# A decoder step: the mask stored in reading order, the last layer's end by halves with filler products, late low parts on DVE alone

## The chip, the cores and the metric

The kernel runs on one core of a Trainium2 chip. The core has a matrix engine (TensorE, PE in the profile), three engines that work on 128 lanes (VectorE = DVE, ScalarE = ACT, GpSimd = POOL) and queues that move data between the chip's memory and SBUF. The engines run at the same time, each its own instructions in a fixed order; a semaphore holds an instruction until its inputs are there. The metric is the time of one execution on the device, in microseconds.

## The reference

Two groups of requests (512 prompt tokens, and 8 requests of 4 new tokens each, behind a cache of 2048) pass through two layers. Cut to what bears on this change:

```python
def trunk_layer(h, pe, pos, attn_fn, ...):
    z = h @ w_in
    a_u, a_v, q, k, v, qi, ki, wi = jnp.split(z, SPLIT_POINTS, axis=-1)
    ...
    b_out = attn_fn(q, k, v, qi, wi, ki)        # index scores, top-k keys, softmax
    mix = jnp.concatenate([a_out, b_out], axis=-1) @ w_o
    h = layer_norm(ALPHA * h + mix, ln1_g, ln1_b)
    ff = jnp.square(jax.nn.relu(h @ w_ff1)) @ w_ff2
    ple = jax.nn.sigmoid(h @ w_ple_gate) * (pe @ w_ple_proj)
    h = layer_norm(ALPHA * h + ff + ple, ln2_g, ln2_b)

def sample_sparse_attn(...):                    # for the 32 sample tokens
    I = indexer_scores(qi, wi, ki_all)          # against 2052 keys
    _, idx = lax.top_k(I, TOPK_SAMPLE)          # 256 of them
    return attend_selected(q, k_sel, v_sel, valid)
```

All is float32, the model width is 1024, the inner width of the MLP 4096.

## The kernel before

The 544 tokens lie as columns, in two halves of 272 (half 0 and half 1), features on the 128 partitions. Each float32 product is three products of rounded operands: a value is split into a high part `hi` (a cast, on ACT, L731) and a low part `lo` = value − `hi` (a subtraction, L735), and `mm3` issues hi·hi, lo·hi and hi·lo, 272 columns each. In the profile these carry the lines 828 to 833 (`mm`, `mm3`); here they are called bulk products. The first MLP matrix uses seven products for eight on 2 x 2 blocks; its operands (`Ah`, `Al`, `Bh`, `Bl`, `w` and `u` in the rows) are sums of the normalised columns that DVE, ACT and POOL make when a half's normalisation ends (L1929 and around).

Every weight comes as a chunk of 128 x 1024, by a DMA (`raw`); `splits` makes `hi` and `lo`. A chunk has a flag `g`, which the kernel before does not read: `Alt` at L734 lets the scheduler choose DVE (V) or POOL (G) for each low part.

The order of all instructions is not written out. Generators (`splits`, `backbone`, `s_attn_f`, ...) yield items: an instruction's engine and cost, an event, a buffer from a pool (`Al`), or alternatives. A list scheduler (`Sched`, L91) picks the item with the smallest start less a weight times the priority of its generator; the table `PR` holds these priorities, `WP` and `WO` the weights for PE and for the others, and `BIAS` and `GBIAS` what it adds to an alternative on DVE or POOL before it compares. What it picks is issued to its engine in that order, for good. So PE, like each engine, waits at the head of its row.

A layer goes: input projections and, among them, the index scores, the selection of the keys, softmax of the prompt blocks (`unit`, `head`) and of the sample tokens (`s_attn_f`); the output projection and first normalisation, half by half; the gate matrix `w_g`, in whose place PE works while the normalisation of the second half is made; then first and second MLP matrix in four steps (`STEPS`), and the second normalisation.

*The mask of the sample attention.* `s_scores` (L1358 to L1373) turns the selection into `maskb`, 128 x 513 bf16, 0 or a large negative number. `s_attn_f` lets PE add it to the scores: for four blocks `f`, four groups of four products with a stationary selector `sel` and 128 columns of `maskb`; the columns of one product lie 32 elements apart. A DVE instruction (L1826) takes each group from PSUM and reduces it.

*The end of a layer.* `F2` and `F2L` list outputs c and halves of the second MLP matrix; in the last of the four steps (q == 3) `F2L` gives outputs 0 to 4 in both halves in turn, then 5 to 7 in half 0, and 5 to 7 in half 1. `ln_apply` sums a half's columns with PE (products with `ones`), computes `mu`, `va`, `y` on DVE (tiny instructions, L861), spreads `mu` and `y` by products with `ident` over all partitions, and spawns `ln_col` for eight columns (L951, L953, L959), and in the last layer the stores.

Of the kernel before, what the change touches and what calls it, by code (L numbers as in the profile page):

```python
# [21 lines left out]
L = 2  # L22
# [29 lines left out]
F2L = F2[:7] + tuple(((c,), (h,)) for h in range(2) for c in (5, 6, 7))  # L52
STEPS = ((0, 5), (5, 9), (9, 13), (13, 16))
WARM = 9
GL = 1200.0
WP = 0.698
WO = 10.415
PR = {'q_sample': 10.5, 'free_raw': -0.5, 'gmix': 7.5, 'evac_c1': 11.5, 's_scores': 17.0, 's_block': 14.0, 'mix_b': 3.5, 'load_r': 8.5, 'kidx': 7.5, 's_attn': 3.0, 'evac_au': -2.5, 'head': 1.5, 's_kt': 6.0, 'loads': 3.0, 'evac_q': -4.0, 'sgu_load': 14.0, 's_relu': 1.5, 'mix_a': 14.5, 'setup1': 5.5, 's_attn_f': 12.5, 'gmlp': 4.5, 'unit': 0.0, 'load_pe': -1.5, 'evac_oa': 0.5, 'backbone': -6.5, 'evac_c0': -3.5, 'setup2': -1.5, 'splits': -2.5, 's_qk': 6.0, 'gnorm': 1.0, 'store': 7.0, 'setup': 6.0, 'wout22': 11.5, 'wadd': 12.0, 'mtee': 4.0, 'fin': 0.5, 'wsum': 7.0, 'wcopy': 0.5, 'evac_p': 10.0, 'ln1': 5.0, 'moving': -1.0, 'vload': 15.5, 'split_x': 12.0, 'evac_f2': -1.5, 'warm': 8.0, 'wsplit': 5.0, 'mv': 5.0, 'evac_o': 9.5, 'wout': 11.5, 'ln2': 10.5, 'evac_g': 6.0}
TBS = (3, 1, 2, 0)
BIAS = 65.107  # L60
GBIAS = 505.244
# [176 lines left out]
def cD(n, k=1):  # L238
    return ("V", (n / 0.96 + 70.0) * k, 1)
# [173 lines left out]
def build(tc, I, O, cols):  # L413
# [182 lines left out]
    for l in range(L):  # L596
# [9 lines left out]
        w["p"] = [chunk(I["w_p"][l, c], 1024, True) for c in range(2)]  # L606
# [95 lines left out]
    def splits():  # L702
        for c in splitq:
# [22 lines left out]
            for i, (a, b, le, re) in enumerate(c.parts):  # L726
# [7 lines left out]
                E = G if (yield Alt([cD(b - a)], [cG(b - a)])) else V  # L734
# [173 lines left out]

    def ln_apply(l, which, half, R, st, xi, dst):
# [5 lines left out]
        sq = st["q7", half]  # L915
        yield [("P", 640.0 * k)]
# [5 lines left out]
        S.free(sq)  # L922
        mu = sm(f"mu{half}", [128, 4])
# [327 lines left out]
    def s_scores(y):  # L1251
# [120 lines left out]
        yield [cW(513)]  # L1372
        V.tensor_scalar(y.maskb, rk[:, :513], -NEG, NEG, op0=ALU.mult, op1=ALU.add)  # L1373
# [440 lines left out]
    def s_attn_f(y, f, Pn, mx, nm, su, rs, vg, ob, fin):  # L1814
        for h2 in range(2):
            for qd in range(2):
                p = yield Al("at", [128, 512])
                yield [("P", 810.0)]
                mk = y.maskb[:, :512].rearrange("p (g h o t) -> p h t o g", h=2, o=8, t=2)
                for t4 in range(4):  # L1820
                    mm(p[:, t4 * 128:t4 * 128 + 128].rearrange("p (o g) -> p o g", o=8), sel[:, f, t4, :],
                       mk[:, h2, qd], True, True)
# [323 lines left out]
    def backbone():  # L2146
        for y in LY:
# [241 lines left out]
            if l + 1 < L:  # L2389
                S.spawn(kidx(LY[l + 1]), 1)  # L2390
# [54 lines left out]
```

## Time and profile before

| | |
|---|---|
| median of 3 runs | 1508.4 us (1508.12 to 1509.75) |
| the profiled execution's own time | 1493.62 us |
| its span, first to last instruction | 1491.9 us |
| mean granted TensorE clock | 0.983 |
| PE busy | 1438.7 us, 96% of the span |
| DVE busy | 1080.0 us, 72% |
| ACT busy | 808.5 us, 54% |
| POOL busy | 180.6 us, 12% |

The profile is of one execution, in microseconds from its first instruction. PE's share is high all the way; the two MLP stages (about 339 to 727 and 1078 to 1466) hold PE without a gap, and what PE idles lies in the attention stages, at the gate matrix, and at the end. In a timeline row, the number in brackets is how long the engine stood idle ahead of the instruction, and what released it; "x8" says that a row stands for eight instructions of one kind, with the time from the start of the first to the end of the last. Matmuls overlap, so what one costs is the distance from start to start.

### The profile page before, as it was taken

The page shows a single profiled execution, that of the slowest core. Times are in us where ns is not written, and L with a number is a line of the kernel's source. Part 1 is how long each engine was busy: PE and PEld are TensorE (multiplying, and loading weights), DVE is VectorE, ACT ScalarE, POOL GpSimd, SP SyncE. Part 2 cuts the span into 40 slices and gives each one's busy share as a digit, 9 for nine tenths or more (in the row PEclk, how much of TensorE's full clock was granted, in tenths as well). Part 3 has the DMA queues.
Part 4 walks back from the last instruction along what each step waited for, and adds up shares of the span by engine and source line. Part 5 has one row for each costly group of instructions (what it writes and reads, how often), then busy time and mean ns, then how long its engine had stood idle before and what let it go on. Part 6 is the DMA issues. An engine that isn't in the chain of part 4 may idle for free.

```text
span 1491.9 us, 31190 instructions
## 1 busy us (share of the span) xinstructions
PE 1438.7 (96%) x12262; PEld 1373.3 (92%) x12262; DVE 1080.0 (72%) x2807; ACT 808.5 (54%) x1893; POOL 180.6 (12%) x204
## 2 busy tenths in 40 slices
PE   9999999899999999999999998999899999999996
PEld 8798878899999999999987998779899999999996
DVE  5699976695955748566676999757869567484765
ACT  6678755473743616344466775754547345172543
POOL 2113511040000000000102044121400000000000
PEclk9999989999999999999999999999999999999998
DMA  7636424112231322313345354151122313222221
GB/s 239 216 100 221 131 100 175 41 43 86 99 128 57 128 72 85 127 58 117 113 129 181 102 198 144 71 187 34 68 72 100 128 58 114 84 101 100 72 71 61
DMA packets 55476, 164.48 MB, mean 110 GB/s; under 512 B 7648, under 2 KB 15008, under 8 KB 55328
## 3 DMA queue, kind: packets, MB, share of 16 engines
q1 hardware_dynamic: 44960, 124.73, 24.7%
q0 software_dynamic: 10368, 37.75, 7.5%
q8 instruction: 96, 1.57, 0.4%
q14 instruction: 52, 0.43, 0.1%
HBM read 156.09 MB, written 6.37 MB: 109 GB/s over the span
## 4 chain that ended last, share of the span: by engine, by line
PE 79%; DVE 11%; ACT 3%; DMA 3%; issue 2%; POOL 1%; POOLq 1%; SPq 0%; ACTq 0%; DVEq 0%
PE at L828 39%; PE mm L828 36%; DVE u L1235 2%; DVE m L1233 2%; PE at L1601 1%; PE at L1693 1%; DMA w<-in_cv,idxV 1%; POOLq L2427 1%; POOL lo L735 1%; DVE lo L735 1%; DMA raw<-in_w_au 1%; DVE t L953 1%; DVE t L951 1%; ACT hi L731 1%; DMA raw<-in_w_c 1%
## 5 line engine op out<-in xcount | busy, mean ns | idle before, releaser
L731 ACT CAST hi<-raw 128x1024 fp32r<-128x1024 f32 (+5 forms) x137 | 138.8, 1019 | 181.4 <-PE mm L828 93.4
L735 DVE TENSOR_TENSOR lo<-raw,hi 128x1024 fp32r<-128x1024 f32 (+5 forms) x131 | 155.6, 1189 | 30.2 <-ACT hi L731 29.6
L828 PE MATMUL mm<-Ah,hi 128*128 128x272 f32 x584 | 172.6, 296 | 0.9 <-DVE u L1899 0.4
L828 PE MATMUL mm<-Bh,hi 128*128 128x272 f32 x584 | 171.8, 294 | 1.5 <-DVE t L1014 1.3
L828 PE MATMUL mm<-Al,hi 128*128 128x272 f32 x584 | 169.4, 290 | 0.0
L828 PE MATMUL mm<-Bl,hi 128*128 128x272 f32 x584 | 168.9, 289 | 0.0
L828 PE MATMUL mm<-Ah,lo 128*128 128x272 f32 x584 | 168.8, 289 | 0.0
L828 PE MATMUL mm<-Bh,lo 128*128 128x272 f32 x584 | 168.6, 289 | 0.0
L828 PE MATMUL at<-w,hi 128*128 128x272 f32 x704 | 158.9, 289 | 0.0
L690 ACT CAST hi<-u 128x512 fp32r<-128x512 f32 x128 | 75.8, 619 | 97.0 <-PE mm L828 40.8
L828 PE MATMUL at<-w,lo 128*128 128x272 f32 x416 | 120.2, 289 | 0.0
L828 PEld LDWEIGHTS at<-w,hi 128*128 128x128 f32 x704 | 119.5, 188 | 0.0
L2073 DVE TENSOR_TENSOR u<-u,mm 128x272 f32<-128x272 f32 x96 | 41.9, 437 | 103.1 <-PE mm L828 102.9
L828 PEld LDWEIGHTS mm<-Bh,hi 128*128 128x128 f32 x584 | 110.7, 190 | 3.1 <-ACT wi L1145 1.7
L828 PEld LDWEIGHTS mm<-Ah,hi 128*128 128x128 f32 x584 | 110.7, 190 | 2.2 <-DVE u L1899 0.5
L690 ACT CAST hi<-raw 128x1024 fp32r<-128x1024 f32 x64 | 53.2, 831 | 109.2 <-PE at L828 35.4
L828 PEld LDWEIGHTS mm<-Ah,lo 128*128 128x128 f32 x584 | 110.8, 190 | 0.2
L828 PEld LDWEIGHTS mm<-Bh,lo 128*128 128x128 f32 x584 | 110.6, 189 | 0.1
L828 PEld LDWEIGHTS mm<-Al,hi 128*128 128x128 f32 x584 | 110.4, 189 | 0.0
L828 PEld LDWEIGHTS mm<-Bl,hi 128*128 128x128 f32 x584 | 110.2, 189 | 0.0
L828 PE MATMUL at<-Al,hi 128*128 128x272 f32 x376 | 108.8, 289 | 0.0
L828 PE MATMUL at<-Bl,hi 128*128 128x272 f32 x376 | 108.8, 289 | 0.0
(392 smaller groups left out, 4384.0 us busy)
## 6 DMA issues: line engine op xcount, KB each, us to landing
raw<-in_w_f SPq DMA_DIRECT2D x128, 512.0 KB, 3.3
raw<-in_w_q SPq DMA_DIRECT2D x16, 512.0 KB, 4.8
raw<-in_w_o SPq DMA_DIRECT2D x16, 512.0 KB, 3.4
raw<-in_w_g SPq DMA_DIRECT2D x16, 512.0 KB, 3.4
raw<-in_w_au SPq DMA_DIRECT2D x8, 512.0 KB, 3.4
raw<-in_w_av SPq DMA_DIRECT2D x8, 512.0 KB, 6.2
u<-in_x SPq DMA_DIRECT2D x8, 272.0 KB, 4.9
hD<-t SPq DMA_DIRECT2D x16, 136.0 KB, 4.2
```

Source lines behind the costliest of these rows:

```text
L690: A.copy(hi[:, :n], x)
L731: A.copy(c.hi[:, a:b], c.raw[:, a:b])
L735: E.tensor_tensor(c.lo[:, a:b], c.raw[:, a:b], c.hi[:, a:b].bitcast(F32), op=ALU.subtract)
L828: PE.matmul(out, l, r, start=start, stop=stop, skip_group_check=True)
L951: V.tensor_tensor(t[:, :n], r[:, a:b], pa[:, :n], op=ALU.subtract)
L953: V.tensor_tensor(t[:, :n], t[:, :n], pb[:, :n], op=ALU.mult)
L1233: V.max(m8, work[:, :N])
L1235: V.match_replace(work[:, :N], m8, work[:, :N], -3.3e38)
L1601: PE.transpose(p[:, c * 128:(c + 1) * 128], P[:, c * 128:(c + 1) * 128], ident)
L1693: PE.transpose(p[:, t, :], raw[:, (g * 4 + t) * 128:(g * 4 + t + 1) * 128], ident)
L2073: V.tensor_tensor(r[:, a:b], r[:, a:b], ps[:, :n], op=ALU.add)
L2427: with tile.TileContext(nc) as tc:
```

## The change

Five edits, two of which only reorder. (1) `PR`, `WP`, `WO` and `GBIAS` get other numbers, so the scheduler makes another order. (2) `maskb` is written in the order in which the products read it: two DVE instructions of 256 columns, read at a stride of 32 elements and written in a row, and one of a single column; the products then read 128 neighbouring columns. (3) In the last layer's last step, outputs 4 to 7 (not 5 to 7) go half by half (`F2E`). (4) `fill` issues products whose result nobody reads (`sel` by 512 columns of `maskb`): ten behind the last output of the last layer, and twelve when the sums of its last half are issued. (5) A low part may go to POOL only for chunks whose flag `g` is set; the flag goes from `w_p`, so DVE makes the low parts of `w_o`, `w_p`, `w_g`, and of the second MLP matrix.

```diff
+F2E = F2[:5] + tuple(((c,), (h,)) for h in range(2) for c in (4, 5, 6, 7))
-WP = 0.698
-WO = 10.415
-PR = {'q_sample': 10.5, 'free_raw': -0.5, ...
+WP = 0.928
+WO = 10.5
+PR = {'q_sample': 13.5, 'free_raw': 8.0, ...
-GBIAS = 505.244
+GBIAS = 422.464
-        w["p"] = [chunk(I["w_p"][l, c], 1024, True) for c in range(2)]
+        w["p"] = [chunk(I["w_p"][l, c], 1024) for c in range(2)]
...
-                E = G if (yield Alt([cD(b - a)], [cG(b - a)])) else V
+                E = G if c.g and (yield Alt([cD(b - a)], [cG(b - a)])) else V
+                if not c.g:
+                    yield [cD(b - a)]
...
+    def fill(pw, n, back):
+        for _ in range(n):
+            yield [("P", 215.0)]
+            mm(pw, sel[:, 0, 0, :], LY[0].maskb[:, :512], True, True)
+        if back is None:
+            S.free(pw)
+
     def ln_apply(l, which, half, R, st, xi, dst):
...
+        end = dst is not None and xi is None and half == 1
+        if end:
+            pw = yield Al("mm", [128, 512])
...
         S.free(sq)
+        if end:
+            S.spawn(fill(pw, 12, None), 0)
...
-        yield [cW(513)]
-        V.tensor_scalar(y.maskb, rk[:, :513], -NEG, NEG, op0=ALU.mult, op1=ALU.add)
+        src = rk[:, :512].rearrange("p (g h o t) -> p h t o g", h=2, o=8, t=2)
+        dst = y.maskb[:, :512].rearrange("p (h t o g) -> p h t o g", h=2, o=8, t=2)
+        for h in range(2):
+            yield [cX(256)]
+            V.tensor_scalar(dst[:, h], src[:, h], -NEG, NEG, op0=ALU.mult, op1=ALU.add)
+        yield [("V", 70.0, 1)]
+        V.tensor_scalar(y.maskb[:, 512:513], rk[:, 512:513], -NEG, NEG, op0=ALU.mult, op1=ALU.add)
...
-                mk = y.maskb[:, :512].rearrange("p (g h o t) -> p h t o g", h=2, o=8, t=2)
                 for t4 in range(4):
-                    mm(p[:, t4 * 128:t4 * 128 + 128].rearrange("p (o g) -> p o g", o=8), sel[:, f, t4, :],
-                       mk[:, h2, qd], True, True)
+                    mm(p[:, t4 * 128:t4 * 128 + 128], sel[:, f, t4, :],
+                       y.maskb[:, (2 * h2 + qd) * 128:(2 * h2 + qd + 1) * 128], True, True)
...
-                for cs, hs in F2L if q == 3 else F2:
+                for cs, hs in F2 if q < 3 else F2E if l == L - 1 else F2L:
...
             if l + 1 < L:
                 S.spawn(kidx(LY[l + 1]), 1)
+            else:
+                pw = yield Al("mm", [128, 512])
+                yield from fill(pw, 10, None)
```

The changed file is longer, so its lines have higher numbers: L735 is L738 there, L861 L864, L951 L966, L1601 L1621, L1929 L1948, L2087 L2106.

*POOL at the gate matrix of layer 0.* POOL's order before (`lo688` and `lo753` are low parts of chunks of `w_g`, `Bl` operands of the first MLP matrix):

```order
L1929 TENSOR_TENSOR u657_4084<-u390_2547,w656_4083 128x272
L1929 TENSOR_TENSOR u657_4084<-u391_2550,w656_4083 128x272
L735 TENSOR_TENSOR lo688_4241<-raw592_3693,hi686_4233 128x1024
L1929 TENSOR_TENSOR u658_4085<-u395_2582,w656_4083 128x272
L1929 TENSOR_TENSOR Bl655_4082<-u390_2547,Bh654_4081 128x272
L1929 TENSOR_TENSOR Bl655_4082<-u391_2550,Bh654_4081 128x272
L1929 TENSOR_TENSOR Bl655_4082<-u392_2559,Bh654_4081 128x272
L735 TENSOR_TENSOR lo753_4645<-raw676_4199,hi736_4514 128x1024
```

and now:

```order
L1948 TENSOR_TENSOR u657_4086<-u370_2427,w656_4085 128x272
L1948 TENSOR_TENSOR u657_4086<-u371_2429,w656_4085 128x272
L1948 TENSOR_TENSOR u658_4087<-u374_2444,w656_4085 128x272
L1948 TENSOR_TENSOR u658_4087<-u378_2460,w656_4085 128x272
L1948 TENSOR_TENSOR Bl655_4084<-u370_2427,Bh653_4082 128x272
L1948 TENSOR_TENSOR Bl655_4084<-u371_2429,Bh653_4082 128x272
L1948 TENSOR_TENSOR Bl655_4084<-u374_2444,Bh653_4082 128x272
L909 TENSOR_TENSOR u1350_8859<-u1350_8859,t1399_9347 128x272
```

Both low parts are gone from POOL; it does one more subtraction of operands.

*DVE at the same place.* Before, from the third low part of `w_g` to the normalisation of half 0 (`y0`: its inverse deviation; L951: the normalisation itself):

```order
L735 TENSOR_TENSOR lo711_4419<-raw603_3771,hi700_4338 128x1024
L2087 TENSOR_SCALAR u712_4428<-mm713_4429 128x272
L861 SCALAR_TENSOR_TENSOR tmp0_4325<-tmp0_4325 92x3
L861 SCALAR_TENSOR_TENSOR y0_4324<-tmp0_4325,y0_4324 92x3
L861 TENSOR_TENSOR tmp0_4325<-y0_4324 92x3
L861 TENSOR_TENSOR tmp0_4325<-tmp0_4325,va0_4323 92x3
L861 SCALAR_TENSOR_TENSOR y0_4324<-tmp0_4325,y0_4324 92x3
L2087 TENSOR_SCALAR u717_4450<-mm718_4451 128x272
L735 TENSOR_TENSOR lo719_4454<-raw667_4153,hi715_4437 128x1024
L951 TENSOR_TENSOR t726_4487<-u390_2547,at721_4471 128x272
```

and now, up to the same place:

```order
L864 SCALAR_TENSOR_TENSOR tmp0_4327<-tmp0_4327,va0_4325 92x3
L864 SCALAR_TENSOR_TENSOR tmp0_4327<-tmp0_4327 92x3
L738 TENSOR_TENSOR lo720_4461<-raw667_4155,hi716_4440 128x1024
L2106 TENSOR_SCALAR u721_4471<-mm722_4472 128x272
L864 SCALAR_TENSOR_TENSOR y0_4326<-tmp0_4327,y0_4326 92x3
L864 TENSOR_TENSOR tmp0_4327<-y0_4326 92x3
L864 TENSOR_TENSOR tmp0_4327<-tmp0_4327,va0_4325 92x3
L864 SCALAR_TENSOR_TENSOR y0_4326<-tmp0_4327,y0_4326 92x3
L738 TENSOR_TENSOR lo732_4508<-raw676_4201,hi726_4494 128x1024
L966 TENSOR_TENSOR t735_4521<-u370_2427,at733_4510 128x272
```

Four low parts, `lo688`, `lo711`, `lo720` and `lo732` (before: two, `lo711` and `lo719`), now stand on DVE ahead of the normalisation; three of them stand between `mu0` and the last step of `y0`, where one stood. On PE the broadcast of `mu0` and `y0` moves from row 1802 of its order to row 1820, and so does that of layer 1, from 6908 to 6926; the product that reads the last low part (`lo753`, now `lo732`) stays at row 1961.

*PE at the mask of layer 0.* Before, two mask groups (of four, of which the last and the first product are shown) and the transposes between them:

```order
L828 LDWEIGHTS sel_111
L828 MATMUL at479_3027<-maskb_137,sel_111 128x128
L1435 MATMUL at477_3019<-identR_106,u357_2318 128x128 x4
L828 LDWEIGHTS sel_111
L828 MATMUL at480_3034<-maskb_137,sel_111 128x128
```

and now:

```order
L831 MATMUL at475_3046<-maskb_137,sel_111 128x128
L1621 MATMUL at478_3063<-ident_101,u461_2932 128x128 x2
L1455 MATMUL at477_3050<-identR_106,u409_2650 128x128 x4
L831 MATMUL at476_3048<-u450_2914,u3_127 64x128
L831 MATMUL at476_3048<-u452_2916,u3_127 64x128
L831 MATMUL at479_3065<-u451_2915,u3_127 64x128
L831 MATMUL at479_3065<-u453_2917,u3_127 64x128
L831 LDWEIGHTS sel_111
L831 MATMUL at480_3071<-maskb_137,sel_111 128x128
```

816 bulk products of the layer stand ahead of the first mask product of 128 columns, and 774 before. Between it and the transposes of the sample tokens' softmax stood 27 before, and none stands now, nor between these and the products with the values. In layer 1 some 70 bulk products that stood ahead of the mask stand in and behind it now.

*PE at the end.* Before, the last of the sums of half 1 and the broadcasts:

```order
L828 MATMUL at2814_18719<-ones_99,u2132_13757 92x1
L828 MATMUL at2814_18719<-ones_99,u2759_18137 92x1
L828 MATMUL at2814_18719<-ones_99,t2813_18713 92x1
L828 MATMUL at2815_18744<-ident_101,mu1_4108 128x92 x3
L828 MATMUL at2816_18745<-ident_101,y1_4110 128x92 x3
```

and now, the last fillers ahead of the broadcasts and one behind them:

```order
L831 MATMUL mm2816_18729<-maskb_137,sel_111 128x512
L831 LDWEIGHTS sel_111
L831 MATMUL mm2813_18720<-maskb_137,sel_111 128x512
L831 MATMUL at2817_18768<-ident_101,mu1_4110 128x92 x3
L831 MATMUL at2818_18769<-ident_101,y1_4112 128x92 x3
L831 LDWEIGHTS sel_111
L831 MATMUL mm2813_18720<-maskb_137,sel_111 128x512
```

Of the 22 fillers, seven stand between the last bulk product and the sums, 13 between the sums and the broadcasts, and two behind.

## Rows read from the trace of the kernel before

**Rows 1.** Part 1 of the page: each engine's busy time, share and instructions.

```profile
PE 1438.7 (96%) x12262; PEld 1373.3 (92%) x12262; DVE 1080.0 (72%) x2807; ACT 808.5 (54%) x1893; POOL 180.6 (12%) x204
```

**Rows 2.** What PE waited for: in all us, times, longest us.

```profile
PE mm L828 <- POOL lo L735: 10.8, 2, 5.4
PE at L1601 <- DVE u L1597: 7.0, 6, 3.3
PE at L828 <- DVE maskb L1373: 1.6, 1, 1.6
```

**Rows 3.** Timeline of POOL in layer 0: start us, us, engine, line, out<-in.

```profile
301.66 2.37 POOL L735 TENSOR_TENSOR lo<-raw,hi 128x1024 fp32r<-128x1024 f32 x1
324.34 14.46 POOL L735 TENSOR_TENSOR lo<-raw,hi 128x1024 fp32r<-128x1024 f32 x1 [5.32 <-ACT hi L731]
```

**Rows 4.** Timeline of PE in layer 0; in brackets the idle time and its releaser.

```profile
338.85 0.60 PE L828 MATMUL mm<-w,lo 128*128 128x272 f32 x1 [5.39 <-POOL lo L735]
```

**Rows 5.** Windows of layers 0 and 1: us, busy us by engine, granted clock, DMA.

```profile
324.00:334.00 10.00, 9.46 (x76) 9.24 (x74) 10.00 (x30) 4.80 (x14) 9.66 (x1) 1.00 0.00 0
339.00:343.00 4.00, 4.00 (x22) 4.00 (x23) 0.00 (x0) 0.00 (x0) 0.00 (x0) 0.65 0.71 261
1077.45:1083.45 6.00, 6.00 (x30) 6.00 (x31) 0.08 (x1) 0.51 (x2) 0.00 (x0) 0.58 0.52 179
```

**Rows 6.** Timeline of DVE in the gate stage of layer 0.

```profile
305.51 0.14 DVE L861 TENSOR_SCALAR mu<-at 92x3 f32<-92x3 f32 x1
309.38 1.22 DVE L735 TENSOR_TENSOR lo<-raw,hi 128x1024 fp32r<-128x1024 f32 x1
311.63 0.16 DVE L861 SCALAR_TENSOR_TENSOR y<-tmp,y 92x3 f32<-92x3 f32 x1
```

**Rows 7.** Timeline of PE in the same stage: half 0's broadcast of the mean.

```profile
312.25 0.80 PE L828 MATMUL at<-ident,mu 92*128 92x92 f32 x6
```

**Rows 8.** Timeline of PE, mask products (layer 1) and transposes (layer 0), with their successors.

```profile
209.03 0.79 PE L1435 MATMUL at<-identR,u 128*128 128x128 f32 x8
209.66 0.36 PE L828 MATMUL mm<-Ah,hi 128*128 128x272 f32 x1
956.29 1.90 PE L828 MATMUL at<-maskb,sel 128*128 128x128 bf16 x8
958.02 0.61 PE L1601 MATMUL at<-ident,u 128*128 128x128 f32 x4
```

**Rows 9.** Window of layer 0's mask products.

```profile
198.00:210.00 12.00, 12.00 (x68) 9.62 (x67) 8.95 (x29) 6.07 (x13) 0.00 (x0) 0.57 0.00 1
```

**Rows 10.** Timeline of DVE ahead of the mask, layers 0 and 1.

```profile
191.59 2.32 DVE L1367 SCALAR_TENSOR_TENSOR u<-u,rem,t 128x513 f32<-128x513 f32 x1
194.67 0.43 DVE L1373 TENSOR_SCALAR maskb<-u 128x513 bf16<-128x513 f32 x1
930.12 0.75 DVE L1367 SCALAR_TENSOR_TENSOR u<-u,rem,t 128x513 f32<-128x513 f32 x1
```

**Rows 11.** Timeline of PE at the end: sums and broadcasts of both halves.

```profile
1463.90 0.57 PE L828 MATMUL at<-ones,u 128*92 128x1 f32 x6
1465.64 0.30 PE L828 MATMUL at<-ones,t 128*92 128x1 f32 x2
1468.89 0.80 PE L828 MATMUL at<-ident,mu 92*128 92x92 f32 x6
1476.49 0.94 PE L828 MATMUL at<-ones,u 128*92 128x1 f32 x6 [1.59 <-DVE u L904]
1479.44 1.59 PE L828 MATMUL at<-ident,mu 92*128 92x92 f32 x6 [0.25 <-DVE mu L861]
1481.37 1.59 PE L828 MATMUL at<-ident,y 92*128 92x92 f32 x6 [0.34 <-DVE y L861]
```

**Rows 12.** Timeline of PE, products of 512 columns and one, layer 1.

```profile
927.07 0.38 PE L828 MATMUL at<-t,gall 128*128 128x512 f16 x2
927.31 0.38 PE L828 MATMUL at<-t,gneg 128*128 128x512 f16 x2
```

More of the change, by code (lines that the diff above doesn't have):

```diff
@@ L55 @@
 GL = 1200.0
-WP = 0.698
-WO = 10.415
-PR = {'q_sample': 10.5, 'free_raw': -0.5, 'gmix': 7.5, 'evac_c1': 11.5, 's_scores': 17.0, 's_block': 14.0, 'mix_b': 3.5, 'load_r': 8.5, 'kidx': 7.5, 's_attn': 3.0, 'evac_au': -2.5, 'head': 1.5, 's_kt': 6.0, 'loads': 3.0, 'evac_q': -4.0, 'sgu_load': 14.0, 's_relu': 1.5, 'mix_a': 14.5, 'setup1': 5.5, 's_attn_f': 12.5, 'gmlp': 4.5, 'unit': 0.0, 'load_pe': -1.5, 'evac_oa': 0.5, 'backbone': -6.5, 'evac_c0': -3.5, 'setup2': -1.5, 'splits': -2.5, 's_qk': 6.0, 'gnorm': 1.0, 'store': 7.0, 'setup': 6.0, 'wout22': 11.5, 'wadd': 12.0, 'mtee': 4.0, 'fin': 0.5, 'wsum': 7.0, 'wcopy': 0.5, 'evac_p': 10.0, 'ln1': 5.0, 'moving': -1.0, 'vload': 15.5, 'split_x': 12.0, 'evac_f2': -1.5, 'warm': 8.0, 'wsplit': 5.0, 'mv': 5.0, 'evac_o': 9.5, 'wout': 11.5, 'ln2': 10.5, 'evac_g': 6.0}
+WP = 0.928
+WO = 10.5
+PR = {'q_sample': 13.5, 'free_raw': 8.0, 'gmix': 7.5, 'evac_c1': 14.0, 's_scores': 17.0, 's_block': 17.5, 'mix_b': 4.5, 'load_r': 6.5, 'kidx': 7.5, 's_attn': 5.0, 'evac_au': -2.5, 'head': 1.5, 's_kt': 6.0, 'loads': 7.5, 'evac_q': -4.0, 'sgu_load': 13.5, 's_relu': 1.0, 'mix_a': 14.5, 'setup1': 8.5, 's_attn_f': 10.5, 'gmlp': 4.5, 'unit': 9.0, 'load_pe': 13.0, 'evac_oa': -0.5, 'backbone': -5.5, 'evac_c0': -3.5, 'setup2': -2.0, 'splits': -2.5, 's_qk': 3.5, 'gnorm': 3.0, 'store': 3.0, 'setup': 13.0, 'wout22': 11.5, 'wadd': 12.0, 'mtee': 4.0, 'fin': 0.5, 'wsum': 7.0, 'wcopy': 0.5, 'evac_p': 10.0, 'ln1': 2.0, 'moving': 11.5, 'vload': 2.5, 'split_x': -1.0, 'evac_f2': 0.0, 'warm': 7.5, 'wsplit': 6.0, 'mv': 5.0, 'evac_o': 9.5, 'wout': 11.5, 'ln2': 10.5, 'evac_g': 0.0}
 TBS = (3, 1, 2, 0)
 BIAS = 65.107
-GBIAS = 505.244
+GBIAS = 422.464
 DMARGIN = 1200.0
@@ L1817, in s_attn_f @@
                 p = yield Al("at", [128, 512])
-                yield [("P", 810.0)]
-                mk = y.maskb[:, :512].rearrange("p (g h o t) -> p h t o g", h=2, o=8, t=2)
+                yield [("P", 300.0)]
                 for t4 in range(4):
-                    mm(p[:, t4 * 128:t4 * 128 + 128].rearrange("p (o g) -> p o g", o=8), sel[:, f, t4, :],
-                       mk[:, h2, qd], True, True)
+                    mm(p[:, t4 * 128:t4 * 128 + 128], sel[:, f, t4, :],
+                       y.maskb[:, (2 * h2 + qd) * 128:(2 * h2 + qd + 1) * 128], True, True)
                 sv = y.S[:, f, h2, qd * 4:qd * 4 + 4].rearrange("p a b c -> p (a b c)")
```

## Prediction

> **What bounds the kernel now.** I first read the busy shares and then what TensorE (PE) waits for, since PE is busy 1438.7 us of the span of 1491.9 us [rows 1]. The reader is to see there that only 53 us of the span are PE's to win back, and that anything else must make PE's own products shorter. The list of PE's waits shows one big entry: two waits of 5.4 us each, for a low part (`lo`) that POOL makes at L735; the others are for DVE and far smaller [rows 2].
>
> The timeline of POOL shows what this low part is. The same instruction, 128 rows by 1024 columns, takes 2.37 us at 301.66 and 14.46 us at 324.34 [rows 3]. While it runs in its long form, DVE is busy 10.00 us of 10 [rows 5], with subtractions and sums that read two operands from SBUF. PE stands in its fixed order before the product that reads this low part and starts again at 338.85 [rows 4]. The windows behind it show a second price: the granted clock, 1.00 while PE streamed, is 0.65 in the mean over the 4 us after the first stall, and 0.58 over the 6 us after the second, in layer 1 [rows 5]; a mean between the levels of 1.2 and 2.4 GHz.
>
> The other places that the change touches: the mask products, eight of which take 958.02 − 956.29 = 1.73 us, 0.216 us each, where eight transposes of as many columns take 209.66 − 209.03 = 0.63 us, 0.079 each [rows 8]; and the end, where PE waits for DVE three times and runs its broadcasts at 1.59 us where the half before took 0.80 [rows 11].
>
> **Low parts on DVE only.** Removed: both stalls, 2 × 5.39 = 10.8 us [rows 2, 4], and the slow clock behind them, 4 × (1 − 0.65) = 1.4 us and 6 × (1 − 0.58) = 2.5 us [rows 5]. Together −14.7. Added: in each layer DVE makes two more low parts, at 1.22 us each [rows 6], and they stand, with two more evacuations of a product, between `mu0` and the last step of `y0`. For an evacuation I estimate 0.35 us, by 272 of the 1024 columns of a low part. That chain took 311.63 − 305.51 = 6.1 us before [rows 6]. Now it gets 2.4 + 0.7, less one subtraction (0.35) that moves out: 2.7 to 2.8 us longer, so `y0` ends near 314.5. The first broadcast of `mu0` and `y0` started at 312.25 [rows 7], and the new order puts 18 products ahead of it, at 0.13 us each (76 in 10 us, [rows 5]) 2.3 us. It then comes to 314.6, and its second half, which is what needs `y0`, some 0.6 us later. So the longer chain is just covered: I take a wait of 0.5 us in each layer. If the cover is gone altogether, the 2.7 us stand bare in both layers, +5.4. Term: −14.7 + 1.0 = **−13.7**, with ends −9.3 and −14.7. What is late next is DVE: `lo732` now stands ahead of the normalisation of half 0, and what this half feeds begins 2.3 us later; but PE reads `lo732` only at its row 1961, as it did `lo753`, 141 rows behind the broadcast, about 19 us.
>
> By the Trainium skill ("SBUF — State Buffer", Who interferes with whom) DVE and GpSimd share one pair of ports as an exclusive lock, and a DVE instruction with two SBUF inputs keeps a GpSimd instruction that reads SBUF out altogether. The 14.46 against 2.37 us agrees. By that rule the four POOL subtractions (L1948) that stay in the stage would now meet the four low parts on DVE, and each could be kept out for one of them, 1.22 us.
>
> **The mask in reading order.** 64 of the 80 mask products read 128 columns a long way apart. Read in a row they should cost what the transposes do, which are fp32r and not bf16, but the nearest rows: 64 × (0.216 − 0.079) = 8.8 us if PE sets the pace and has the full clock. PE does set it in layer 0: it is busy 12.00 us of 12 from 198 to 210, at a mean granted clock of 0.57 [rows 9]. But DVE, which takes each group of four with a reduction, is busy 8.95 of these 12 us [rows 9]: it allows 3.0 us in layer 0 at most, while its work stays in the stretch. In layer 1 products of the projections stand between, and 32 × 0.137 = 4.4 can nearly all be had; I take 3.5. Term: **−6.5**; the ends are 0 (DVE sets the pace everywhere) and −11 (8.8, and 2 us of clock).
>
> The write of the mask becomes two instructions of 256 columns and one of one column in place of one of 513 at 0.43 us [rows 10]. From that row, and 0.16 for the smallest DVE instructions (the last of `y0`, [rows 6]), 0.43 + 0.16 + 0.16 makes +0.3 a layer on a chain for which PE already waited 1.6 us once [rows 2]. In that chain stood also the one instruction of 2.32 us whose twin in layer 1 took 0.75 [rows 10]; a POOL low part ran beside it, and this goes, −1.6 in layer 0. In layer 1 the order now puts some 70 bulk products less between the selection and the mask: I give back 0.5 there. Term **−0.6**, from −1.6 to +3.
>
> The skill's page "SBUF — State Buffer" (SBUF "cachelines", under Door 1: The DMA port swizzle) says that accesses that leave a 16-byte line each pay. DVE now reads the mask at a stride of 32 fp32 values, as PE did before. By the rule DVE would pay there what PE saves: at PE's own ratio of 0.216 to 0.079 the write grows from 0.43 to 1.2 us. The trace before has no such DVE read, so it can only be bounded; the upper end of +3 covers two of them with both waits.
>
> **The last layer's end.** The last product ends at 1476.49 − 1.59 = 1474.90; the sums start 1.59 later, the broadcast of `mu` at 1479.44 takes 1.59, that of `y` starts at 1481.37 and takes 1.59, so it ends at +8.06 [rows 11]. The clock falls in between. The nearest row for a filler is a pair of 512 columns and one: 927.31 − 927.07 = 0.24 [rows 12], so 0.215 for 512. Seven stand before the sums: 1.5 us, as long as the wait they fill. The sums take 2.0, as they did for the half before, from 1463.90 to 1465.94 (for this half 2.95, at a falling clock) [rows 11], to +3.5. Then 13 more stand ahead of the broadcast, since PE keeps its order: 2.8 us, to +6.35, when `mu` and `y` are there already (from the end of the sums to the broadcast of `y` DVE took 1.9 us, so `y` is there by +5.5). With two broadcasts of 0.80, as for the half before [rows 11], the end is at +7.95. Term **−0.1**: the fillers hold the broadcast up by as much as the clock gives back. The far end: the clock falls all the same, 13 × 0.43 + 2 × 1.59, +4. The half-by-half order of four outputs moves no product off PE; it only lets half 0's normalisation end 3 us earlier.
>
> **The new order.** Nothing of PE's amount of work changes except 22 fillers. In layer 0, 42 bulk products stand ahead of the mask that stood in or behind it: 5 us of cover that the softmax chains between mask and outputs no longer have, but one of the waits of those chains (7.0 us in six waits [rows 2]) lies at the very end, and units that start earlier shorten it. I take 0, ±5.
>
> Sum: −13.7 − 6.5 − 0.6 − 0.1 = −20.9. The profiled execution's own time is 1493.62 us (1491.9 and 1.7 around it), so 1472.7 for such an execution. It is 14.8 us under the median of the runs shown, and I carry that distance on: 1508.4 − 20.9 = 1487.5, **1488**.
>
> **Rivals.**
> A, DVE becomes the bound at the gate. `y0` misses its broadcast by 2.7 us in both layers, or the POOL subtractions are kept out for as long: for it, DVE is full from 324 to 334; against it, the 18 products. −9.3 for the term, 1492.
> B, the mask products were not PE's pace: the reductions on DVE (busy 75% there [rows 9]) take their place, and the term is near 0: −14.4, 1494.
> C, the attention loses its cover. In layer 0 no bulk product stands between the first mask product and the value products; PE, in order, waits at the transposes of a softmax that DVE has not scaled. That is the wait of 3.3 us that stands once now [rows 2]; it decides when it comes some six times more in the two layers, 21 us, which eats all: 1508 to 1514. For it, DVE's chains are long and 42 and some 70 products left; against it, the same products are still done somewhere, and cover waits that exist.
> D, the low part on POOL was only the last of several late things, and PE meets another 3 us later: each stall keeps 2 to 3 us of its 5.4, and the clock falls all the same: 1498.
>
> **How the numbers follow.** The forecast within ±4: 0.45. A 0.15, B 0.15, D 0.10, C 0.07, and 0.08 for more than the forecast (clock and order both give). The range 1475 to 1501 leaves out C and the ends of the others, some 0.15 to 0.2. A difference under 0.2%, 3 us, is about what a measurement of this kernel cannot tell from none. Faster by more: all but C and a mixture of D with lost cover, 0.87. Within 0.2%: 0.06. Slower: 0.07.
>
> **What the changed profile would show.** Right: no PE wait on POOL at L738, the granted clock 1.00 from 333 to 345; PE's wait for `y` in the broadcast under 1 us; mask products at 0.08 us; a broadcast of `mu` at 0.8 us near the end, starting right behind a filler. Wrong: a wait of PE on DVE `y` or `Bl` of 2 us and more in the gate stage (A), mask groups that follow each other at DVE's 0.7 us (B), new waits at L1621 of 3 us (C), broadcasts at 1.59 us again in the end.

## The result: 1471.8 us, below the range

The changed kernel takes 1471.76 us in the median (1470.9 to 1472.45, four runs) against 1508.88 (1508.12 to 1509.75) for the kernel before: a ratio of 0.9758, with a 95% interval of 0.9742 to 0.9774. The forecast was 1488 with a range of 1475 to 1501: the direction was right, the gain of 37 us is 1.8 times the 20.9 forecast. The profiled executions tell another story: 1493.62 before and 1471.24 after, 22.4 us apart, 1.5 us from the sum. The changed kernel's profiled execution stands at its median; that of the kernel before stood 15 us below its own. So the sum as a whole held for the execution from which it was read, and what went wrong is how it was carried to the median. Most of what follows is about these 15 us.

First the page of the changed kernel, its line of busy times and that of the chain that ended last (before, DVE had 11% of that chain and POOL 1%):

```profile
PE 1427.5 (97%) x12284; PEld 1363.9 (93%) x12284; DVE 1083.2 (74%) x2812; ACT 805.4 (55%) x1895; POOL 143.8 (10%) x201
PE 79%; DVE 15%; ACT 3%; issue 1%; DMA 1%; another core or an unknown queue 0%; SPq 0%; DVEq 0%; ACTq 0%
```

and two of PE's waits (us in all, times, longest), the largest and the only one on a low part:

```profile
PE at L1621 <- DVE u L1617: 4.6, 3, 3.3
PE mm L831 <- DVE lo L738: 0.9, 2, 0.5
```

No wait on POOL is left. At the two gate matrices, where [rows 2] had 10.8 us, PE does not wait for a low part at all; the 0.9 us are two waits in the input projections, at 123.4 and 850.0 us, and come with the new order (b_tables, below, has them too). PE is busy 11 us less than in [rows 1].

The gate stage of layer 0, PE's broadcast first, then the last step of `y0` and the last low part on DVE:

```profile
312.24 0.80 PE L831 MATMUL at<-ident,mu 92*128 92x92 f32 x6
312.87 0.83 PE L831 MATMUL at<-ident,y 92*128 92x92 f32 x6
312.12 0.16 DVE L864 SCALAR_TENSOR_TENSOR y<-tmp,y 92x3 f32<-92x3 f32 x1
313.03 1.23 DVE L738 TENSOR_TENSOR lo<-raw,hi 128x1024 fp32r<-128x1024 f32 x1 [0.75 <-ACT hi L732]
```

They answer to [rows 6, 7]. `y0` ends at 312.28, and the broadcast that needs it starts at 312.87: the longer chain is covered by the 18 products, with 0.6 us to spare. The broadcast stands at the same instant as before with 18 products more ahead of it, so PE came to this stage 2.3 us earlier. `mu0` came as much earlier (303.24, before 305.51), and the chain from it to the end of `y0` takes 9.0 us where it took 6.3: the 2.7 to 2.8 us more of the forecast. The windows behind answer to [rows 5]:

```profile
326.00:333.00 7.00, 7.00 (x57) 6.84 (x56) 7.00 (x21) 3.83 (x10) 0.00 (x0) 1.00 0.00 0
333.00:345.00 12.00, 12.00 (x97) 11.95 (x96) 10.83 (x21) 5.35 (x8) 0.00 (x0) 1.00 0.48 146
1063.00:1080.00 17.00, 17.00 (x137) 17.00 (x137) 12.09 (x22) 4.98 (x11) 0.00 (x0) 1.00 0.45 149
```

The granted clock stays at 1.00 through both gate stages, though DVE is as full ahead of layer 0's as before (7.00 us of 7).

The mask of layer 0, answering to [rows 8, 10]: eight mask products and what follows on PE, then on DVE the instruction that took 2.32 us and the new write of the mask, and the wait that PE has some microseconds later:

```profile
203.83 0.62 PE L831 MATMUL at<-maskb,sel 128*128 128x128 bf16 x8
204.28 0.39 PE L1621 MATMUL at<-ident,u 128*128 128x128 f32 x2
186.49 0.76 DVE L1382 SCALAR_TENSOR_TENSOR u<-u,rem,t 128x513 f32<-128x513 f32 x1
188.49 0.75 DVE L1391 TENSOR_SCALAR maskb<-u 128x256 bf16<-128x256 f32 x2
189.16 0.14 DVE L1393 TENSOR_SCALAR maskb<-u 128x1 bf16<-128x1 f32 x1
212.90 1.85 PE L1621 MATMUL at<-ident,u 128*128 128x128 f32 x12 [3.32 <-DVE u L1617]
```

Eight products take 204.28 − 203.83 = 0.45 us, 0.056 each, where they took 0.216. (By the Trainium skill, "TensorE: Matmul & The Clock Gate", Wait — 56ns, not 53.3ns?, products of 128 columns follow each other at about 55.6 ns at full clock; the trace agrees.) The write of the mask went from 0.43 to 0.75 + 0.14, 0.4 to 0.5 us more, where the sum had 0.3. The wait of 3.32 us on a scaled softmax is the longest one of [rows 2]; it stood at 263.2 us and now stands nearer to the mask.

The end, answering to [rows 11], on PE and then DVE's first L968:

```profile
1453.97 0.57 PE L831 MATMUL at<-ones,u 128*92 128x1 f32 x6
1458.68 0.80 PE L831 MATMUL at<-ident,mu 92*128 92x92 f32 x6
1459.32 0.83 PE L831 MATMUL at<-ident,y 92*128 92x92 f32 x6
1460.22 0.78 DVE L968 TENSOR_TENSOR t<-t,at 128x272 f32<-128x272 f32 x2
```

The sums begin at +1.36 behind the last bulk product (1452.61), the broadcasts take 0.80, as forecast, and that of `y` ends at +7.54 (before +8.06).

A table of stages shows where the rest is. Its times are differences between instants: the start of the span, PE's first broadcast of a mean in each layer, the first product of layer 1, the end of the last bulk product, the end of the span. The second and the fourth column are other executions of the two kernels (b_again2 and a_again, below):

| stage, us | before, profiled | before, another | after | after, another |
|---|---|---|---|---|
| attention, layer 0 | 294.2 | 298.7 | 291.9 | 294.5 |
| gate and MLP, layer 0 | 441.6 | 443.1 | 435.0 | 435.0 |
| attention, layer 1 | 296.9 | 304.5 | 289.3 | 290.3 |
| gate and MLP, layer 1 | 442.1 | 442.6 | 436.4 | 436.3 |
| end | 17.0 | 16.8 | 16.9 | 16.9 |

The gate stages gave 6.6 and 5.7, or 8.1 and 6.2: 12.3 to 14.3 us, the 13.7 of the sum. The attention gave 2.3 and 7.6 against the profiled execution (9.9, forecast 7.1), but 6.8 and 15.2 against the other one. Of the 14 us between the two columns of the kernel before, 12.1 lie in its attention stages.

### The profile page after: what moved, and what is told of

Read it like the earlier page. It is cut to its first block, busy times and chain, and to the rows that moved or that the text cites. A ratio compares the mean times of both kernels' runs of the same rounds, so it can differ in the third digit from the quotient of the medians.

```text
span 1469.5 us, 31243 instructions
## 1 busy us (share of the span) xinstructions
PE 1427.5 (97%) x12284; PEld 1363.9 (93%) x12284; DVE 1083.2 (74%) x2812; ACT 805.4 (55%) x1895; POOL 143.8 (10%) x201
## 4 chain that ended last, share of the span: by engine, by line
PE 79%; DVE 15%; ACT 3%; issue 1%; DMA 1%; another core or an unknown queue 0%; SPq 0%; DVEq 0%; ACTq 0%
PE at L831 40%; PE mm L831 36%; DVE u L1250 3%; DVE m L1248 3%; DVE lo L738 1%; PE at L1621 1%; DVE u L1607 1%; DVE t L968 1%; PE at L1880 1%; DVE c L1336 1%; DVE u L1577 0%; DVE t L966 0%; PE at L1713 0%; DMA Bh<-in_x 0%; DVE w L868 0%
## 5 line engine op out<-in xcount | busy, mean ns | idle before, releaser
L738 DVE TENSOR_TENSOR lo<-raw,hi 128x1024 fp32r<-128x1024 f32 (+5 forms) x136 | 161.9, 1190 | 36.3 <-ACT hi L732 35.7
L691 ACT CAST hi<-raw 128x1024 fp32r<-128x1024 f32 x64 | 53.2, 831 | 104.2 <-PE at L831 35.5
```

The costliest lines, as they stand in the source:

```text
L691: A.copy(hi[:, :n], x)
L738: E.tensor_tensor(c.lo[:, a:b], c.raw[:, a:b], c.hi[:, a:b].bitcast(F32), op=ALU.subtract)
```

## Experiments

Medians are in us; each is compared with the kernel before on the same chip, run between. Five chips took part. The kernel before was at 1510.8, 1501.3, 1510.5, 1502.3 and 1511.1 on them, the changed kernel at 1474.4 on the third and 1472.9 on the fifth.

**What the 15 us are: b_again, b_again2.** The kernel before, unchanged.

> The kernel before, unchanged. Its profiled execution took 1493.62 us, its timed executions 1508.4 in the median: 15 us that the profile did not have, while the changed kernel's profiled execution (1471.24) stands at its median (1471.76). Theory T1: the 15 us are the two low parts that POOL makes beside DVE; how long POOL is kept out differs from execution to execution (14.46 us in the profiled one, some 7 us more each in the others). Then an execution of about 1508 us shows POOL low parts of about 22 us at L735 and two PE waits of about 12.5 us. Theory T2: the 15 us lie elsewhere (clock of the MLP stages, mask stretch, attention), and the low parts take 14.5 us in every execution.

b_again: 1504.6 (1503.6 to 1509.8). Its profiled execution, 1509.84 us, is the kind that the first profile had missed. POOL's low parts (durations in ns: least, median, most):

```profile
L735 POOL TENSOR_TENSOR lo<-raw,hi x6: 2364/2380/14461, 194.8 to 1078.9; 128x1024 fp32r<-128x1024 f32 x6
```

three of PE's waits:

```profile
PE mm L828 <- POOL lo L735: 10.8, 2, 5.4
PE at L828 <- issue: 4.1, 6, 1.0
PE at L1861 <- issue: 1.2, 2, 1.0
```

and two windows, columns as in [rows 5]:

```profile
345.00:352.00 7.00, 5.83 (x25) 5.83 (x26) 0.00 (x0) 0.15 (x1) 1.12 (x1) 0.51 0.41 150
1011.00:1015.00 4.00, 1.83 (x18) 0.98 (x14) 0.29 (x2) 1.02 (x3) 1.88 (x2) 0.90 0.99 391
```

T1 falls: the longest low part took 14.461 us here as well, and PE waits for it 10.8 us. T2 stands. What is new are PE's waits on 'issue' (it waited for nothing that the profile shows), 5.3 us on these two lines. The longest stand where the DMA engines are full, as in the second window (0.99, 391 GB/s). The same products in the two executions, b_again first,

```profile
1011.38 0.56 PE L828 MATMUL at<-u,u 128*64 128x128 f32 x6 [0.26 <-issue]
1012.85 0.44 PE L828 MATMUL at<-u,u 128*64 128x128 f32 x4 [0.91 <-issue]
1014.29 0.80 PE L828 MATMUL at<-u,u 128*64 128x128 f32 x5 [1.00 <-issue]
```

and the first profile:

```profile
997.01 2.19 PE L828 MATMUL at<-u,u 128*64 128x128 f32 x36
```

36 products of 64 rows stream in 2.2 us in the first profile and stand three times, 2.2 us in all, in b_again. Full DMA engines alone do not bring this: the first profile has 1.03 and 406 GB/s from 1000 to 1003 us and no wait on 'issue' anywhere. Nor is the changed kernel free of such waits: 2.4 us in its profile, 3.1 in a_again, 4.1 in a_again2. The first window shows the second part: the low clock behind the stall lasts longer, 0.51 in the mean over 7 us, where [rows 5] had 0.65 over 4. Over all, PE was idle 53.2 us from the start of the span to its last product in b_again, 53.0 in b_again2, 44.3 in the first profile, and 33.1 in the changed kernel.

> The kernel before once more, for the chip: with 'issue' waits of PE (4 to 5 us in b_again) the median is 1508 to 1511 as on the first chip; without them 1501 as on the second. If the granted clock alone decides, the executions lie on one line: some 1.4 us for each 0.001 of the clock's mean.

b_again2, third chip: 1511.0 (1503.7 to 1513.9), with 5.9 us of waits on 'issue'. Its ten executions of 1503.7 to 1513.9 had mean granted clocks from 0.986 down to 0.975, the slower ones lower, with a scatter of some 3 us. But the clock does not part the chips: at 0.983 the kernel before took 1495.30 on the fourth chip, 1504.22 on the first and 1507.42 on the third, which is b_again2's profiled execution. On the second and fourth chips, at 1501 to 1502, the profiles of the kernel's relatives (b_tail, b_gate, b_mask2, b_gate2) show no such wait. So part of the difference between chips is these waits; why some chips have them is open. Of 74 other executions of the kernel before, none was below 1495.3: the 1493.62 of the first profile was the shortest of all. But with its clock of 0.983 and no wait on 'issue' it lies beside the executions of the second and fourth chips. The record does not say on which chip it ran, nor on which the runs of its median did; if on two, the 15 us are in part a distance between chips.

**One low part alone: b_one.**

```diff
+                late = any(c is w["g"][3] for w in W)
-                E = G if (yield Alt([cD(b - a)], [cG(b - a)])) else V
+                E = G if not late and (yield Alt([cD(b - a)], [cG(b - a)])) else V
+                if late:
+                    yield [cD(b - a)]
```

> The kernel before with one low part of each layer (chunk 3 of w_g, the one that took 14.46 us) on DVE; every other low part may go to POOL as before. T1: both the stall and the 15 us go: 1508.9 - 13 - 15 = 1481, with the profiled execution within 3 us of the median. T2: only the stall as the profile had it goes: 1508.9 - 13 = 1496, with the profiled execution still some 15 us under it. If PE then meets another thing that is late: 1500 and more.

1503.7 against 1510.8, −7. Both theories had more. PE's wait changed its name, and not by much:

```profile
PE mm L831 <- DVE lo L738: 6.4, 2, 3.2
```

DVE makes the low part in 1.2 us, but the old priorities put it behind the normalisation of half 0 and the operands that follow, and PE still waits 3.2 us in each layer. The engine was 2.2 of the 5.4 us of the stall; its place in DVE's order is the rest. This is rival D for this one edit.

**The mask alone: b_mask, b_mask2.** Edit 2 as in the change.

> The kernel before with the mask in reading order alone (written by two instructions of 256 columns and one of one, read in a row). The prediction's term: -6.5 for the products and +0.3 a layer for the write, so 1502 to 1503. T2 with the mask as the place of the 15 us: about 1488. If DVE sets the pace there: 1508.

> Edit 2 alone once more. On the first chip it gained 8.8; taken away from the changed kernel it cost 8.4. -8 to -9 here, with PE's busy time some 10 us less and its idle time unchanged.

b_mask: 1502.0 against 1510.8, −8.8; b_mask2, on the fourth chip: 1490.2 against 1502.3, −12.1. The busy lines of b_again, then b_mask:

```profile
PE 1445.9 (96%) x12262; PEld 1377.2 (91%) x12262; DVE 1078.5 (72%) x2807; ACT 809.2 (54%) x1893; POOL 180.8 (12%) x204
```

```profile
PE 1434.6 (96%) x12262; PEld 1371.5 (92%) x12262; DVE 1078.9 (72%) x2814; ACT 806.5 (54%) x1889; POOL 184.1 (12%) x205
```

PE is busy 11.3 us less, 6.9 and 5.3 less in the two attention stages (in part by less time at the low clock), and its idle time is the same (53.2 and 53.4). So the products were PE's pace in both layers, and rival B falls.

**Low parts on POOL in the new order: a_pool.** Edit 5 undone in the changed kernel.

> The changed kernel with the choice of DVE or POOL given back to all low parts; in the order that follows, POOL makes two of the low parts of w_g in each layer, but both ahead of the normalisation of half 0, where DVE's second operands lie in PSUM, not after it. If POOL's being kept out by two-operand work of DVE is the cause: no stall, low parts of 2.4 us, and 1472 +- 3. If low parts on POOL cost PE whatever stands beside them: 1485 to 1500.

1476.4 (before: 1510.8). POOL makes seven low parts, two of `w_g` in each layer among them:

```profile
L736 POOL TENSOR_TENSOR lo<-raw,hi x7: 2361/2373/2407, 299.0 to 1043.1; 128x1024 fp32r<-128x1024 f32 x7
```

None takes over 2.41 us and PE waits for none. The slowest stands beside a full DVE, too, but beside the normalisation, whose second operand `at` lies in PSUM (the products' output memory) and not in SBUF:

```profile
312.71 2.41 POOL L736 TENSOR_TENSOR lo<-raw,hi 128x1024 fp32r<-128x1024 f32 x1 [10.58 <-ACT hi L732]
313.03 0.78 DVE L966 TENSOR_TENSOR t<-t,at 128x272 f32<-128x272 f32 x2
```

So it is not a busy DVE but its work with two operands from SBUF that makes a low part on POOL take 14.46, as was expected. Edit 5 adds some 2 to 5 us to the new order (the changed kernel was at 1471.8 to 1474.4, but on other chips).

**Edit 5 alone: b_gate, b_gate2.**

> The kernel before with edit 5 alone: low parts of chunks without the flag on DVE only, the scheduler's old tables. Here the last low part of w_g stands on DVE ahead of the normalisation of half 0, as in the changed kernel (in b_one it stood behind it, and PE still waited 3.2 us for it in each layer). The prediction's term: -13.7 against the kernel before on the same chip, no PE wait on L737 over 1 us and clock 1.00 behind row 1961. Rival: other low parts that leave POOL load DVE in the attention, where DVE is the bound, and give half of it back: -7.

> Edit 5 alone once more, beside b_mask2 and b_gm on one chip. On the second chip it gained 17 against 13.7 forecast. If what the profiled execution of before did not show (low clock, waits on 'issue') hangs on the two stalls: -17 to -20 here too. If it depends on the chip: -14 where the kernel before is at 1501, more where it is at 1510.

1484.4 against 1501.3 (−16.9) and 1484.8 against 1502.3 (−17.5), on the second and fourth chips. The gate and MLP stages fall to 435.2 and 436.0 us, as in the changed kernel. That is −14. Where the other 3 us lie is not shown. The attention of layer 0 takes 295.1 and 295.2 us, where b_again, b_again2 and b_tail take 298.7 to 302.5, and PE is idle 15 us there and not 19 to 20; but the first profile had 294.2, and 15 us idle, with all its low parts on POOL. Here the rival fails: with −17 and not −7, fewer low parts on POOL did not slow the attention.

**The order alone: b_tables.** Edit 1 in the kernel before.

> The kernel before with edit 1 alone (PR, WP, WO, GBIAS). In this order POOL makes its two late low parts of w_g ahead of the normalisation, so the 14.46 us low part should be gone as well. The prediction gave the order itself 0 +- 5, which with the stall gone makes -14 +- 5 against the kernel before. Theory T3: executions of the kernel before differ (1493.6 to 1514 us) by stretches at the low clock and by PE waits on 'issue' in the attention stages, and an order with fewer gaps has fewer of both: -20 or more, and a spread under 5 us. Rival T4: the spread is the chip's and the same for every kernel: then the spread stays 10 us and more.

1477.5 against 1501.3, −23.8. PE has no wait on the gate's low parts here either, since POOL makes them early: the gate and MLP stages take 434.7 and 434.9 us, and b_tail's on the same chip 443.0 and 442.6, 16 of the 24. The rest is order: PE is idle 32.6 us in all, though with the mask read as before the attention of layer 0 had a granted clock of only 0.96. The spread, 1472.0 to 1479.0, is not under 5 us; T4's 10 us it is not either.

**The end alone: b_tail.** Edits 3 and 4 in the kernel before.

> The kernel before with edits 3 and 4 alone: four outputs by halves and 22 fillers in the end. The prediction's term: -0.1, 'held up by as much as the clock gives back' (from -1 to +4). If the fillers keep the clock at full speed and the end of the last product is followed 7.5 us later by the last normalisation: -0.5. Broadcasts of 0.80 in place of 1.59 us in either case, unless the clock falls all the same (+4).

1503.6 against 1501.3, a ratio of 1.0004 with the interval from 0.9986 to 1.0021: nothing. The broadcasts take 0.80 and the one of `y` ends at +7.8.

**All but the order: a_oldtables; both parts that count: b_gm.**

> The changed kernel with the old tables (edits 2 to 5 without 1). If the order is worth nothing beside the other edits, as the prediction took it: 1472 +- 5. T3: the old order keeps its gaps, low clock and issue waits in the attention: 1480 to 1490, and a spread of some 10 us as before.

> Edits 5 and 2 together, old tables, old end. If the two add up: -26 against the kernel before on this chip. If they share what they save (the same low clock): -20. If the changed kernel's whole gain of some 36 us lies in these two: within 2 us of 1472, and the order and the end are worth nothing in sum; else the order brings the rest, up to 10 us.

a_oldtables: 1473.7 against 1501.3, −27.6. b_gm: 1472.9 against 1502.3, −29.4, which is, to 0.2, the −17.5 and −12.1 of the two single edits beside it, added. Both are within 2 us of the changed kernel on other chips. So beside these two edits no gain of order and end shows: T3's share for the order falls, though the order alone gets most of the way too, by another road. The changed kernel itself did not run on these two chips, where the kernel before is 9 us quicker; as it has 2.4 to 4.1 us of waits on 'issue' elsewhere, and neither of these two has any, a gain of the order of that size is not excluded.

**From the side of the changed kernel: a_again, a_oldmask.**

> The changed kernel again, on the chip of the three runs beside it. On two chips the kernel before had medians of 1510.8 and 1501.3 us, and its executions differed by 6 to 10 us on each. If this spread comes with stretches at the low clock and waits behind gaps that the change removes: 1472 +- 2, spread under 4 us, granted clock 0.990 or more, whatever the kernel before does here. If the chip sets it: the changed kernel moves with the kernel before, by up to 10 us.

> The changed kernel with the mask stored and read as before. The prediction's terms for the mask, -6.5 and -0.6: +7.1 against the changed kernel. b_mask, with the old order, gained 8.8 in the median, with a longer stretch at the low clock gone: +9. If the new order had moved the mask products out of the way anyway: +2 or less.

On the third chip a_again took 1474.4 (1473.3 to 1476.4), where the kernel before took 1510.5, a_oldmask 1482.8: the mask is worth 8.4 here. Busy lines of a_again, then a_oldmask:

```profile
PE 1430.1 (97%) x12284; PEld 1364.9 (93%) x12284; DVE 1083.5 (74%) x2812; ACT 805.8 (55%) x1895; POOL 143.6 (10%) x201
```

```profile
PE 1439.9 (97%) x12284; PEld 1368.5 (92%) x12284; DVE 1086.3 (73%) x2808; ACT 807.1 (54%) x1895; POOL 145.3 (10%) x201
```

9.8 us of PE's time, all of it in the attention stages.

**The fillers: a_nofill, a_again2, a_nofill2, a_fill4.**

```diff
-            S.spawn(fill(pw, 12, None), 0)
+            S.free(pw)                        # a_nofill; a_fill4: fill(pw, 4, None)
-                yield from fill(pw, 10, None)
+                S.free(pw)                    # a_nofill; a_fill4: fill(pw, 2, None)
```

> The changed kernel without its 22 fillers (the four outputs by halves stay). The prediction's term gives them 0 (they hold the broadcasts up by as much as the clock gives back): 0 to +0.5 against the changed kernel on this chip, broadcasts of 1.59 us, the broadcast of y ended some 7.8 to 8.1 us behind the last bulk product. If the end without them starts at the low clock, as in b_gate (9.2 us): +1 to +1.6.

> The changed kernel, as the reference of the two beside it: 1471 to 1475.

> No fillers, the four outputs by halves kept. On the third chip it was 3.7 us under the changed kernel: 0.9 of it in the end (the last normalisation started at +6.7 behind the last bulk product in place of +7.6, since the fillers hold the broadcast of mu up by 3 us and the clock gives back only 2), and 2.8 by less time at the low clock in layer 0, which fillers in layer 1's end cannot reach. If only the end is theirs: -0.9 against a_again2. If it is 3 us again, the fillers change something ahead.

> Two fillers ahead of the sums and four behind in place of ten and twelve. If few are enough to keep the clock: broadcasts of 0.80 us, last normalisation at about +6 behind the last bulk product, -1.5 against a_again2. If the clock falls as without any: +7.2, no better than a_nofill2.

a_nofill: 1470.7 against a_again's 1474.4. On the fifth chip a_again2, a_nofill2 and a_fill4 took 1472.9, 1472.1 and 1472.0. So the 3.7 did not come again. On the third chip the four executions of the one (1468.8 to 1471.0) do not reach those of the other (1473.3 to 1476.4); in the profiles the attention of layer 0, ahead of any filler, takes 290.3 against 294.5 us. Why is open. On the fifth chip the medians cannot tell these kernels apart, but the profiles can. Without fillers, the broadcasts on PE and the first L968 on DVE:

```profile
1455.81 1.59 PE L831 MATMUL at<-ident,mu 92*128 92x92 f32 x6 [0.25 <-DVE mu L864]
1457.74 1.59 PE L831 MATMUL at<-ident,y 92*128 92x92 f32 x6 [0.34 <-DVE y L864]
1459.36 0.79 DVE L968 TENSOR_TENSOR t<-t,at 128x272 f32<-128x272 f32 x2 [0.97 <-PE at L831]
```

and with six:

```profile
1459.28 0.80 PE L831 MATMUL at<-ident,mu 92*128 92x92 f32 x6
1460.73 0.90 PE L831 MATMUL at<-ident,y 92*128 92x92 f32 x6 [0.65 <-DVE y L864]
1461.67 0.78 DVE L968 TENSOR_TENSOR t<-t,at 128x272 f32<-128x272 f32 x2 [0.29 <-PE at L831]
```

The last bulk product ended at 1452.69 and 1455.88. The last normalisation then starts at +6.67 without fillers, with broadcasts of 1.59 (a_nofill2: +6.18), at +5.79 with six, with broadcasts of 0.80 and 0.90, and at +7.61 with 22 [the end, above]; in the kernel before it started at +8.10 and, in b_again2, at +7.80. Without any the sums start at once (two of them even ahead of the last product's end), since half 0's normalisation no longer stands ahead of the evacuation on DVE; b_tables, with the new order and the old end, still waits 1.58 us there. So the four outputs by halves give 1.1 to 1.9 us, and the 22 fillers take 0.9 to 1.4 of it back. a_fill4 is 1.8 us ahead of the changed kernel in the end, 2.0 to 2.3 ahead of the kernel before, and 0.9 ahead of a_again2 in the median, inside the spread.

## Why the prediction was wrong

The step that failed is the last of the sum: "It is 14.8 us under the median of the runs shown, and I carry that distance on". It took the distance for something that both kernels have. The runs show it in the kernel before only: its other executions took 1495.3 to 1515.0 us, while the changed kernel's all lie within 6 us of each other, and its profile at its median. What such a distance is made of shows in b_again2, 13.8 us longer than the first profile at the same mean granted clock of 0.983: 8.7 us are idle time of PE, all of it in the attention stages and part of it waits on 'issue' (5.9 us, where the first profile has none); in the other 5 us PE is busy, and why longer was not taken apart. From the profiled execution itself the sum gave 1472.7, 0.9 us from the median measured. That it came so near is in part luck: from profile to profile the gate and MLP stages gave 1.4 us less than their term and the attention 2.8 more than its own. And where the kernel before is at 1501 to 1502, the low parts and the mask alone gave 17 and 12 us, some 9 more than their terms. Since the profile could not say which of the two times it would be, the range should have held both, 1472.7 and 1487.5, with what lies around each.

By its steps:

- *Low parts on DVE*, −13.7: −12.3 from profile to profile, −14 in the gate and MLP stages against other executions, as b_gate shows. The cover was as worked out, and the wait of 0.5 us a layer that the term allowed for did not come. The price of the clock, read as 1.4 and 2.5, is what the stages gave beyond the stalls of 5.4: 1.2 and 0.3 against the first profile, 2.7 and 0.8 against b_again2. b_gate's −17 in the median holds some 3 us more that the term did not have; which of the moved low parts gives them was not taken apart.
- *The mask*, −6.5 and −0.6: −8.4, −8.8 and −12.1. The term was mis-sized twice. The nearest row, transposes at 0.079, is not what such a product costs, 0.056: 64 × 0.160 = 10.2, not 8.8. And the limit that I took from DVE's busy time in layer 0 (3.0 us) did not hold, since the orders made for the cheaper products put other work beside it: in b_gm, with the old tables, bulk products stand between the mask groups, and PE and DVE are both busy 8.00 us of 8 from 198 to 206. The write, reading at a stride, took 0.75 us for the two halves where the prediction let it grow to 1.2 at PE's ratio: the stride costs DVE much less than it cost PE. (That ratio was the prediction's own; the Trainium skill, "SBUF — State Buffer", SBUF "cachelines", gives a penalty for each access that crosses to a new 16-byte line and no size for it; the trace agrees that there is one: 256 columns read at the stride take 0.41 us here, and 0.29 where DVE's L1253 reads 256 in a row.)
- *The end*, −0.1: −0.1 from the last product to the last instruction. The sum was right, its parts were opposite: the order by halves gives 1.1 to 1.9 and the fillers take 0.9 to 1.4 back, of which the sum had said that the one "only lets half 0's normalisation end 3 us earlier" and that the other holds the broadcast up "by as much as the clock gives back".
- *The order*, 0: beside the two edits no gain shows, across chips, within some 2 to 4 us.
- *The rivals.* A did not come: PE does not wait for `y` at the gate's broadcast, and the longest POOL subtraction (L1948) takes 1.01 us, before 0.99, so none is kept out for 1.22. B did not come. C did not: PE's idle time in the attention is 32.3 us, 31.2 in the first profile and 40 in b_again and b_again2. D came only in b_one. More than the forecast had 0.08, for clock and order; it came, but not by the order.

What stays open: whether the first profile was an odd execution or an ordinary one of a chip like the second and fourth; why three chips have the kernel before at 1511 and two at 1501 (waits on 'issue', seen on two of the three, are some 6 of these 10 us); and what the changed kernel takes on a chip of the second kind, where it did not run.

## What to carry to other kernels

Before a sum is made against a profiled execution, put that execution beside the median of the timed ones: a distance of 1% is a part of the kernel that the profile does not show, or another chip, and if the change touches the stages with waits, the gain may be the sum or the sum and the distance; say both. A stall behind another engine has two causes, the engine and the place in its order, and moving only the engine may leave half of it. Fillers that keep a clock up must end before what they wait beside is ready: against none, six brought the last normalisation forward by 0.4 to 0.9 us, and 22 put it back by 0.9 to 1.4.

## Not expected of the hardware

The same program, undisturbed, took from 1493.6 to 1515.0 us, up to 11 us apart on one chip and 10 us between the medians of chips, with the mean granted clock from 0.987 to 0.974; the changed one from 1470.9 to 1476.4. PE's small products (0.055 us apart) stand for up to 1.0 us at a time on nothing that the profile shows while the DMA engines are 0.99 busy, in some executions, and in others do not at 1.03. The late low part on POOL took 14.45 to 14.46 us in both layers of six profiles with the old order (the first, b_again, b_again2, b_mask, b_mask2, b_tail), and a low part on POOL elsewhere 2.34 to 2.47. A mask product read at a stride took 0.216 to 0.219 us from start to start both at 1.2 GHz (layer 0 of the first profile) and at 2.4 (layer 1): the stride, and not the clock, was its pace.
